# A channel shuffle on one core: copies on VectorE alone, program order, a small first tile and three small last ones

## The chip, the cores and the metric

The kernel runs on one core of a Trainium2 chip. The metric is the device time of one execution in microseconds (us), lower is better. All runs below are on one core at a granted clock of 1.0.

## The reference

Channels are regrouped: within each row of 256 channels, 8 groups of 32 are transposed to 32 groups of 8. Nothing is computed.

```python
# x: 16 x 64 x 64 x 256, float32; groups = 8
x = x.reshape(batch, h, w, groups, channels_per_group)
x = x.transpose(0, 1, 2, 4, 3)
return x.reshape(batch, h, w, c).astype(np.float32)
```

That is 65,536 rows of 1 KB: 67.11 MB to read and 67.11 MB to write.

## The kernel before

A tile gives each of the 128 partitions q rows, lying together in memory, so that a load or a store moves one run of q KB per partition: a 24-row tile is 3 MB in 128 descriptors of 24,576 bytes, an 8-row tile is 1 MB in 128 descriptors of 8,192 bytes. Loads are issued from SyncE (queue q1 in the profile), stores from ScalarE (queue q10). In between, the permuting copy is split evenly, the first half on VectorE (DVE), the second on ScalarE (ACT).

```python
_SIZES = [24] * 21 + [8]
_IN_BUFS = 4
_OUT_BUFS = 4
_SHARES = (("vector", 1), ("scalar", 1))
# ... (cut: pools, rows(), permute())
    first = 0
    for q in _SIZES:
        in_tile = in_pool.tile([P, biggest * c], F32, name="in_tile")
        nc.sync.dma_start(out=in_tile[:, : q * c], in_=rows(x_flat, first, q))
        out_tile = out_pool.tile([P, biggest * c], F32, name="out_tile")
        # ... (cut: for each engine of _SHARES, its rows of the tile)
                permute(engine, out_tile[:, cols], in_tile[:, cols])
        nc.scalar.dma_start(out=rows(out_flat, first, q), in_=out_tile[:, : q * c])
        first += P * q
```

## Time and profile before

| | before |
|---|---|
| time, median of 3 | 317.53 us (317.53 to 317.59) |
| span of the profile | 316.0 us |
| ACT busy, DVE busy | 119 us (38%), 65 us (21%) |
| bytes moved, rate over the span | 134.2 MB, 425 GB/s |
| DMA engines continuously occupied | from 1.7 to about 313.9 us |

The page of the kernel before shows the busy tenths of each of 40 slices of the span, and then the queues:

```profile
DVE  0440321303030303113030303031220303030310
ACT  1681624425160606243351606061533426060620
...
DMA  8999999999999999999999999999999999999996
...
## 3 DMA queue, kind: packets, MB, share of 16 engines
q1 hardware_dynamic: 3168, 67.11, 49.8%
q10 hardware_dynamic: 3168, 67.11, 49.3%
```

The two compute rows are mostly empty and the DMA row is full, so the 16 DMA engines bound the kernel, loads and stores taking half each. A packet of the profile has the size of one descriptor: each queue has 2,688 of 24,576 bytes (912 ns at the median), 128 of 8,192 bytes (309 ns), and 352 of 4 bytes (9 ns; in all as many as the semaphore updates by DMAs in the trace, 704: the "semaphore packets" of the prediction). So a DMA here has 128 with data and 16 of 4 bytes, and 22 DMAs make 3,168. The listing by form gives the copies, with busy time, mean ns of one, and idle time before them with what ended it:

```profile
L49 ACT COPY out_tile<-in_tile 128x3072 f32<-128x3072 f32 x21 | 115.7, 5510 | 180.3 <-DMA in_tile<-in_x_dram 180.3
L51 DVE COPY out_tile<-in_tile 128x3072 f32<-128x3072 f32 x21 | 64.2, 3058 | 231.6 <-DMA in_tile<-in_x_dram 231.6
```

Both engines wait for loads. A 24-row load takes its share of the DMA for 14.5 us, the slower copy 5.5 us. The end of the timeline (start us, duration, engine, what) shows how it drains:

```profile
292.64 5.43 ACT L49 COPY out_tile<-in_tile 128x3072 f32<-128x3072 f32 x1 [9.11 <-DMA in_tile<-in_x_dram]
...
302.35 1.94 ACT L49 COPY out_tile<-in_tile 128x1024 f32<-128x1024 f32 x1 [4.29 <-DMA in_tile<-in_x_dram]
302.41 2.25 ACTq L66 DMA_DIRECT2D out_dram<-out_tile  x2
```

The last load has come in at 302.3 us; the store of the tile copied at 292.6 to 298.1 us goes out only at 302.4, behind the issue of the next copy. Still the engines stay busy with stores to the end, as the windows view shows (window, its length, busy us of DVE, ACT and POOL with instructions, clock, DMA share, GB/s):

```profile
300.00:308.00 8.00, 1.09 (x1) 1.94 (x1) 0.00 (x0) 1.00 1.03 443
308.00:311.00 3.00, 0.00 (x0) 0.00 (x0) 0.00 (x0) 1.00 0.95 410
311.00:312.00 1.00, 0.00 (x0) 0.00 (x0) 0.00 (x0) 1.00 0.78 328
312.00:313.00 1.00, 0.00 (x0) 0.00 (x0) 0.00 (x0) 1.00 1.04 442
313.00:314.00 1.00, 0.00 (x0) 0.00 (x0) 0.00 (x0) 1.00 0.70 295
314.00:316.00 2.00, 0.00 (x0) 0.00 (x0) 0.00 (x0) 1.00 0.01 4
```

This view books a packet in the window in which it starts, so short windows swing (0.78, then 1.04); with each packet spread over its own duration the engines are 16 of 16 busy up to 313 us.

### The profile page before, as it was taken

What the parts mean: (1) busy time and instruction counts of PE and PEld (TensorE: products, weight loads), DVE (VectorE), ACT (ScalarE), POOL (GpSimd) and SP (SyncE); (2) the same over time, 40 slices, a digit from 0 to 9 for tenths busy, and PEclk for the clock granted to TensorE, in tenths of its full rate; (3) what the DMA queues carried; (4) which work ended last, traced back from release to release, by engine and by line L of the source; (5) the groups of instructions that cost most, each with busy time, mean ns of one, the idle gap of its engine ahead of it and who ended that gap; (6) DMA issues with size and microseconds to landing.
All of it is one profiled execution on the core that took longest, in us unless ns stands there. A gap on an engine that the chain in (4) does not pass through costs nothing.

```text
span 316.0 us, 236 instructions
## 1 busy us (share of the span) xinstructions
DVE 65.3 (21%) x22; ACT 118.9 (38%) x23; POOL 0.2 (0%) x4
## 2 busy tenths in 40 slices
DVE  0440321303030303113030303031220303030310
ACT  1681624425160606243351606061533426060620
POOL 0000000000000000000000000000000000000000
DMA  8999999999999999999999999999999999999996
GB/s 302 439 395 426 426 445 432 420 442 439 417 439 445 417 436 442 426 426 445 426 423 445 439 414 442 442 417 439 442 421 432 442 420 432 442 429 429 421 446 291
DMA packets 6337, 134.23 MB, mean 425 GB/s; under 512 B 704, under 2 KB 704, under 8 KB 704
## 3 DMA queue, kind: packets, MB, share of 16 engines
q1 hardware_dynamic: 3168, 67.11, 49.8%
q10 hardware_dynamic: 3168, 67.11, 49.3%
q14 instruction: 1, 0.01, 0.0%
HBM read 67.11 MB, written 67.11 MB: 425 GB/s over the span
## 4 chain that ended last, share of the span: by engine, by line
another core or an unknown queue 43%; DMA 32%; ACT 20%; ACTq 1%; issue 0%
DMA in_tile<-in_x_dram 32%; ACT out_tile L49 20%; ACTq L66 1%; ACTq L49 0%
## 5 line engine op out<-in xcount | busy, mean ns | idle before, releaser
L49 ACT COPY out_tile<-in_tile 128x3072 f32<-128x3072 f32 (+1 forms) x22 | 117.7, 5348 | 184.6 <-DMA in_tile<-in_x_dram 184.6
L51 DVE COPY out_tile<-in_tile 128x3072 f32<-128x3072 f32 (+1 forms) x22 | 65.3, 2968 | 238.3 <-DMA in_tile<-in_x_dram 238.3
L49 ACT ACT_TABLE_LOAD x1 | 1.3, 1283 | 0.7 <-PEq L84 0.7
L84 POOL MEMSET const-bfloat16-1.0<- 128x1 bf16 x1 | 0.1, 102 | 0.0
L84 POOL MEMSET const-uint8-127<- 128x1 uint8 x1 | 0.1, 102 | 0.0
L84 POOL MEMSET const-float32-1.0<- 128x1 f32 x1 | 0.1, 99 | 0.0
L84 POOL MEMSET const-float32-0.0<- 128x1 f32 x1 | 0.1, 98 | 0.2 <-issue 0.2
## 6 DMA issues: line engine op xcount, KB each, us to landing
in_tile<-in_x_dram SPq DMA_DIRECT2D x21, 3072.0 KB, 52.6
out_dram<-out_tile ACTq DMA_DIRECT2D x21, 3072.0 KB, 20.2
in_tile<-in_x_dram SPq DMA_DIRECT2D x1, 1024.0 KB, 47.9
out_dram<-out_tile ACTq DMA_DIRECT2D x1, 1024.0 KB, 10.4
```

What stands on the lines that cost most here:

```text
L49: nc.scalar.copy(out=dst, in_=src)
L51: getattr(nc, engine).tensor_copy(out=dst, in_=src)
L66: nc.scalar.dma_start(out=rows(out_flat, first, q), in_=out_tile[:, : q * c])
L84: nc = _bacc.Bacc("TRN2", target_bir_lowering=False, num_devices=1)
```

## The change

The intent: ScalarE, which also issues the stores, is freed of copies; every store is issued right after its own copy; a small first tile starts the copies and stores sooner; and small last tiles shorten the drain. The whole diff:

```diff
-_SIZES = [24] * 21 + [8]
+_SIZES = [8] + [24] * 20 + [8, 8, 8]
-_SHARES = (("vector", 1), ("scalar", 1))
+_SHARES = (("vector", 1),)
@@
+    ctx.enter_context(tc.manual_schedule(engines=None))
     first = 0
     for q in _SIZES:
```

The line with `manual_schedule` is the one for the order. There are 48 DMAs in place of 44.

## The prediction

> **What bounds the kernel now.** The DMA engines. The page's slice row shows them at 8 or 9 tenths in every slice but the last, 425 GB/s over the span. Packet by packet, the trace has the 16 engines occupied from 1.7 us to about 313.9 us of a 316.0 us span. A 24,576-byte descriptor (one partition of a 24-row tile) takes 912 ns at the median, loading or storing: 24,576 x 16 / 912 ns = 431 GB/s. The 134.2 MB at that rate are 311 us. The rest is 1.7 us ahead of the first packet, about 1.6 us of slow load packets (each engine's first takes 1.4 to 2.2 us, and a patch near 18 to 22 us runs long), and about 1.5 us after the last store. [...]
>
> The compute engines wait: by form, ACT COPY of 128x3072 takes 5.51 us and DVE 3.06 us, x21 each; in the waits DVE idles 238 us and ACT 185 us for loads. A tile comes every 14.5 us (timeline), so copies are hidden. The chain of waits names ACT for 20%, but the DMA is busy beneath it: worth nothing.
>
> **What the change does.**
> - Removes the ACT copies (118 us) and the 1.3 us table load; DVE takes whole tiles. From its 1.095 us for 1024 elements and 3.02 us for 3072, 0.94 ns per element: about 5.9 us for 6144, 2.05 us for 2048 (estimates). The copy phase goes from 5.43 to 5.9 us inside a 14.5 us period: off the critical path. DVE total about 126 us, 40%.
> - Order. Before, the program puts two ACT copies ahead of two store issues, so every other store, ready 9 us sooner, is issued just after the next copy has started (65.5 to 74.5 us). After, each store follows its own copy. Queueing is shorter, but the queues had work anyway: 0 us.
> - First tile: lands after about 5 us instead of 11.0, first store about 9 us earlier. But the engines are busy with queued loads then: 0 us.
> - Last tiles: the final tile is 8 rows in both. From 302 to 314 us before, stores alone fill the engines. After, I estimate that some 10 us of stores are still queued when loading ends, against about 4 us to land, copy and issue the last tile: no gap, 0 us.
> - 48 DMAs for 44. An 8-row tile has 8,192-byte descriptors at 309 ns: three take 927 ns instead of 912. One 24-row tile cut in three, 8 descriptors per engine, both ways: 8 x 15 ns x 2 = 0.24 us; more 9 ns semaphore packets add 0.04 us. All on the critical path: +0.3 us.
>
> **Prediction.** 317.53 + 0.3 = 317.8 us; 8 in 10 between 317.2 and 318.6. Chances: faster by over 2% 0.01, within 2% 0.97, slower 0.02.
>
> **What would show it.** DMA still 8 or 9 tenths in all middle slices, mean 424 to 426 GB/s; 24,576-byte packets still at 912 ns; DVE COPY 128x6144 at 5.8 to 6.0 us x20; no ACT copy; one store issue after each copy; median landing of stores under 20.2 us; last store packet within 1 us of before's.
>
> **What would make it wrong.** A gap in the DMA row near the end, if stores have run down when the last loads land (some us); packets slower or faster under the more even mix of loads and stores (1% would be 3 us); the slow patch near 20 us going away or growing (0.7 us either way). A different DVE rate is harmless below 14 us.

The sum stands as 317.53 + 0.3 = 317.8 us.

## The result, and the profile after

The changed kernel took 318.53 us (median of 6, 318.35 to 318.63) against 317.56 (6 runs, 317.53 to 317.80) beside it. The ratio is 1.0028, 95% interval 1.0015 to 1.0041. (Ratios here are the mean of one kernel's fast runs over the mean of the other's of the same rounds, so not quite the ratio of the medians.) A second set of five, run later as an experiment, gave 318.42 us and 1.0025. So it is slower by 0.25 to 0.28%: small, but clear of zero.

The page after, in the parts that answer to those above:

```profile
DVE  2256153442607071524426170716244261707222
...
DMA  8999999999999999999999999999999999999996
...
## 3 DMA queue, kind: packets, MB, share of 16 engines
q1 hardware_dynamic: 3456, 67.11, 49.8%
q10 hardware_dynamic: 3456, 67.11, 49.3%
```

ACT has gone and the DMA row has not changed. The 288 more packets per queue are the two additional DMAs of 144 each. By form, DVE now has:

```profile
L51 DVE COPY out_tile<-in_tile 128x6144 f32<-128x6144 f32 x20 | 113.8, 5692 | 170.1 <-DMA in_tile<-in_x_dram 170.1
L51 DVE COPY out_tile<-in_tile 128x2048 f32<-128x2048 f32 x4 | 8.1, 2024 | 20.1 <-DMA in_tile<-in_x_dram 20.1
```

Its 5.69 us per tile is hardly more than ACT's half took before, and it waits for loads still. The difference is at the end. Timeline:

```profile
295.44 2.04 DVE L51 COPY out_tile<-in_tile 128x2048 f32<-128x2048 f32 x1 [4.02 <-DMA in_tile<-in_x_dram]
305.17 2.01 DVE L51 COPY out_tile<-in_tile 128x2048 f32<-128x2048 f32 x1 [7.68 <-DMA in_tile<-in_x_dram]
310.12 2.02 DVE L51 COPY out_tile<-in_tile 128x2048 f32<-128x2048 f32 x1 [2.94 <-DMA in_tile<-in_x_dram]
```

and the same stretch in windows (no ACT column, as ACT does nothing):

```profile
300.00:308.00 8.00, 2.01 (x1) 0.00 (x0) 1.00 0.96 409
308.00:311.00 3.00, 0.88 (x1) 0.00 (x0) 1.00 1.01 426
311.00:312.00 1.00, 1.00 (x1) 0.00 (x0) 1.00 0.41 172
312.00:313.00 1.00, 0.15 (x1) 0.00 (x0) 1.00 0.00 0
313.00:314.00 1.00, 0.00 (x0) 0.00 (x0) 1.00 1.07 451
314.00:316.00 2.00, 0.00 (x0) 0.00 (x0) 1.00 0.74 299
```

From about 311.6 us most DMA engines have nothing to do, and from 312.1 to 313.0 none has: the DMA share falls to 0.00 while DVE ends the copy of the last tile and its store is issued. Packet by packet, the idle time after 290 us up to the end of the first engine to finish is 1.4 us, averaged over the engines; before it is none. The last load packet ends at 309.3 us. The tile is landed and the copy begins at 310.1, ends at 312.1, and the store's first packet starts at 313.0: 3.7 us. But only 2.3 us of stores were left at 309.3. (Stores that are "left" are those of the earlier tiles, in time of the 16 engines together, here and below.)

Why were so few left? The small loads came slowly. A DMA view between 286 and 304 us, in which two of the three 8-row loads run beside 24-row stores (packets, MB, share of the engines' time):

```profile
q10 hardware_dynamic: 254, 5.85, 75.5%
q1 hardware_dynamic: 266, 1.94, 25.5%
```

The queues have had about the same number of packets, 254 and 266, and so very different numbers of bytes. 309 ns of load against 912 ns of store is a share of 309 / (309 + 912) = 25%, and this is what the view shows. It holds the other way round too. From 14 to 20 us the small first tile's 8,192-byte stores run beside 24,576-byte loads, with as many packets again:

```profile
q1 hardware_dynamic: 80, 1.97, 76.0%
q10 hardware_dynamic: 80, 0.66, 25.8%
```

In mid-run of the same kernel, from 200 to 229 us, with 24,576 bytes on both sides, the shares are even:

```profile
q1 hardware_dynamic: 288, 6.29, 50.4%
q10 hardware_dynamic: 287, 6.27, 50.2%
```

### The profile page after: what moved, and what is told of

The parts are those of the page before. It is cut to its first block, busy times and chain, and to the rows that moved or that the text cites. A ratio compares the mean times of both kernels' runs of the same rounds, so it can differ in the third digit from the quotient of the medians.

```text
span 316.9 us, 178 instructions
## 1 busy us (share of the span) xinstructions
DVE 121.9 (38%) x24; POOL 0.2 (0%) x4
## 4 chain that ended last, share of the span: by engine, by line
another core or an unknown queue 39%; DMA 30%; DVE 29%; issue 0%; DVEq 0%; SPq 0%
DMA in_tile<-in_x_dram 30%; DVE out_tile L51 29%; DVEq L51 0%; SPq L57 0%
## 5 line engine op out<-in xcount | busy, mean ns | idle before, releaser
L51 DVE COPY out_tile<-in_tile 128x6144 f32<-128x6144 f32 (+1 forms) x24 | 121.9, 5080 | 190.2 <-DMA in_tile<-in_x_dram 190.2
## 6 DMA issues: line engine op xcount, KB each, us to landing
out_dram<-out_tile ACTq DMA_DIRECT2D x20, 3072.0 KB, 23.6
```

What stands on the lines that cost most here:

```text
L51: getattr(nc, engine).tensor_copy(out=dst, in_=src)
```

## The experiments

Theory A: each DMA engine alternates one descriptor of the load queue with one of the store queue. The starts of the packets in the profile after look like it: 16 load packets start between 297.07 and 297.44 us, 16 store packets between 297.38 and 297.75, each 306 ns after one of those loads, and load packets again from 298.28. (The packets carry no engine number here, so this is read from their starts.) At the end, small loads therefore get a quarter of the time, the large stores three quarters; the stores run out before the last tile is in, and the hole in the DMA row follows. Its rivals: B, the small first tile leaves too little lead; C, program order or VectorE alone; D, the small copies and stores, or the number of DMAs. Runs e1 to e4 ran on one chip, beside 9 runs of the kernel before with median 317.73 us; e5 to e8 together on one chip, beside 11 with median 317.67. All results were correct.

### e1_big_last: no small last tiles

```diff
-_SIZES = [8] + [24] * 20 + [8, 8, 8]
+_SIZES = [8] + [24] * 21
```

> The changed kernel with sizes [8] + [24] x 21: small first tile, no small last ones, 44 DMAs. Theory A (the extra time over the 0.3 us of descriptors is a 1.5 us hole in the DMA row at 312 to 313 us, which is there because the three last loads have 8,192-byte descriptors, each engine alternates one load and one store descriptor, so these loads get a quarter of the time and the stores run down): no loads of small descriptors at the end, so no hole of over 0.5 us, the 16 engines busy to the last store; 317.3 to 317.9 us. Rival B (the small first tile leaves the loads with less lead over the stores for the whole run, and the tail is short of stores for that): the hole stays or is longer, since the last copy is now 5.7 us instead of 2.0; 319 us or more. Rival C (program order and VectorE alone cost it, whatever the sizes): 318.3 to 318.7 as after.

317.24 us (317.15 to 317.38), ratio 0.9988 (0.9975 to 1.0000). No hole to speak of (0.1 us); the last load packet ends at 298.8 us and stores fill the rest. This although the last copy takes 5.7 us:

```profile
300.11 5.68 DVE L51 COPY out_tile<-in_tile 128x6144 f32<-128x6144 f32 x1 [8.82 <-DMA in_tile<-in_x_dram]
```

It was just enough: 7.9 us of stores were left at 298.8, and the last tile's store began 7.9 us later. B has fallen: the small first tile is there and does no harm.

### e2_old_sizes: VectorE and program order, the old sizes

```diff
-_SIZES = [8] + [24] * 20 + [8, 8, 8]
+_SIZES = [24] * 21 + [8]
```

> VectorE alone and program order with the old sizes [24] x 21 + [8]: the copy and order parts of the change by themselves. Theory A: one small last load only, over 6 us of stores are left when it ends, no hole; 317.3 to 317.8 us, as before. Rival C: 318.3 or more.

317.57 us (317.29 to 317.87), ratio 0.9997 (0.9985 to 1.0010): as before. No hole; 10.4 us of stores are left when the last load ends. C has fallen: moving the copies and the order of the stores costs nothing.

### e3_new_sizes_only: both engines and the old order, the new sizes

```diff
 # against the kernel before
-_SIZES = [24] * 21 + [8]
+_SIZES = [8] + [24] * 20 + [8, 8, 8]
```

> The kernel before (both engines, its own order of issues) with the new sizes alone. Theory A: the three small last loads again take a quarter of the engines' time against 24-row stores; a hole of at least 1.5 us near the end, longer than after's if the second-last store is held back behind the last copy; 318.3 to 321 us. Rival C: no hole, 317.8 us (the descriptors' 0.3 us alone).

317.85 us (317.65 to 318.29), ratio 1.0007 (0.9993 to 1.0021). By its time alone this does not differ from the kernel before. There is a hole, but one of 0.8 us and not of 1.5 or more; my expectation was wrong about its size and about the sign of what the old order does to it. Windows of this run (DVE, ACT, POOL):

```profile
308.00:309.00 1.00, 0.00 (x0) 0.00 (x0) 0.00 (x0) 1.00 0.95 401
309.00:310.00 1.00, 0.72 (x1) 0.89 (x1) 0.00 (x0) 1.00 0.12 49
310.00:311.00 1.00, 0.41 (x1) 1.00 (x1) 0.00 (x0) 1.00 1.07 451
```

The second-last store had been ready since 303.3 us, but is issued at 309.2 with the start of the last copies. Held back, it was still to be done when the last tile came in, and filled the engines while that tile was copied: the old order hides a part of the hole by accident.

### e4_cut_stores: the last large stores cut to small descriptors

The loads stay as the change has them. The stores of the last two 24-row tiles are cut.

```diff
+_CUT = (19, 20)  # their stores in three DMAs of 8 rows
-    for q in _SIZES:
+    for n_tile, q in enumerate(_SIZES):
@@
-        nc.scalar.dma_start(out=rows(out_flat, first, q), in_=out_tile[:, : q * c])
+        step = 8 if n_tile in _CUT else q
+        for r in range(0, q, step):
+            cols = slice(r * c, (r + step) * c)
+            nc.scalar.dma_start(out=rows(out_flat, first, q)[:, cols], in_=out_tile[:, cols])
```

> The changed kernel, but the stores of its last two 24-row tiles each go out as three DMAs of 8 rows, so that from about 286 us loads and stores both have 8,192-byte descriptors. Theory A: loads and stores then share the engines about 8 to 8 (not 4 to 12), the last load ends about 299 us instead of 309, over 8 us of stores are left then, the hole is gone, and the time falls although descriptors cost another 0.24 us: 317.7 to 318.2 us. Rivals B and C: the share of loads or the hole does not depend on the size of the store descriptors; 318.6 to 318.9 us (after plus 0.24).

317.68 us (317.55 to 318.08), ratio 1.0003 (0.9990 to 1.0015), although this program has four more DMAs than the changed kernel. The DMA view from 286 to 299 us:

```profile
q10 hardware_dynamic: 373, 2.79, 50.8%
q1 hardware_dynamic: 369, 2.76, 50.2%
```

As many packets from each queue again, and with equal descriptors an even share of bytes. The last load packet ends at 299.6 us in place of 309.3, 12.2 us of stores are left, and the hole is gone:

```profile
308.00:311.00 3.00, 0.00 (x0) 0.00 (x0) 1.00 1.01 426
311.00:312.00 1.00, 0.00 (x0) 0.00 (x0) 1.00 1.01 426
312.00:313.00 1.00, 0.00 (x0) 0.00 (x0) 1.00 1.03 434
```

Nothing about loads, copies or tile sizes was changed; what changed is the size of the descriptors that the loads alternate with.

### e5_after_again: the changed kernel once more

> The changed kernel once more, unaltered, on the same chip as the next three, to compare them directly: 318.3 to 318.7 us, a hole of about 1.5 us in the DMA row near 312 us.

318.42 us (318.37 to 318.59), ratio 1.0025 (1.0012 to 1.0038). The hole is 1.2 us here; 2.4 us of stores were left when the last load ended.

### e6_one_load_three_stores: small copies and stores, no small loads

```diff
-_SIZES = [8] + [24] * 20 + [8, 8, 8]
+_SIZES = [8] + [24] * 21
@@ the load of each tile is one DMA, as before; then
+        step = 8 if n_tile == len(_SIZES) - 1 else q
+        for r in range(0, q, step):
+            cols = slice(r * c, (r + step) * c)
+            out_tile = out_pool.tile([P, biggest * c], F32, name="out_tile")
+            permute("vector", out_tile[:, : step * c], in_tile[:, cols])
+            nc.scalar.dma_start(out=rows(out_flat, first, q)[:, cols], in_=out_tile[:, : step * c])
```

> Sizes [8] + [24] x 21 in program order on VectorE; the last tile is loaded by one DMA of 24 rows, but copied and stored in three pieces of 8 rows: the small tail for copies and stores without the small loads. Theory A: the loads keep 24,576-byte descriptors, so loads and stores share evenly to the end, over 10 us of stores are left when the last load ends, no hole; 317.2 to 317.7 us. Rival D (it is the three small copies and stores, or having 48 DMAs, that cost it, not the small loads): a hole or 318.3 us and more.

317.24 us (317.01 to 317.32), ratio 0.9986 (0.9974 to 0.9998). No hole:

```profile
311.00:312.00 1.00, 0.00 (x0) 0.00 (x0) 1.00 1.01 426
312.00:313.00 1.00, 0.00 (x0) 0.00 (x0) 1.00 1.00 426
```

Its four small copies and four small stores are those of the changed kernel; only the last three loads are one. D has fallen. It is the fastest version here that is clear of the kernel before, by 0.14%; it does not differ from e1.

### e7_three_loads_one_store: the mirror

```diff
-_SIZES = [8] + [24] * 20 + [8, 8, 8]
+_SIZES = [8] + [24] * 21
@@
-        nc.sync.dma_start(out=in_tile[:, : q * c], in_=rows(x_flat, first, q))
+        step = 8 if n_tile == len(_SIZES) - 1 else q
+        for r in range(0, q, step):
+            cols = slice(r * c, (r + step) * c)
+            nc.sync.dma_start(out=in_tile[:, cols], in_=rows(x_flat, first, q)[:, cols])
```

> The mirror of the run before: the last 24-row tile is loaded by three DMAs of 8 rows into one buffer, copied whole and stored by one DMA. Bytes, copies and stores are those of the kernel with sizes [8] + [24] x 21 (317.24 us); only one load is cut. Theory A: the three loads get a quarter of the engines while 24-row stores last (to about 305 us), end at about 306 to 307 us instead of 299, and then a 5.7 us copy and about 1.4 us of landing and issue come with no store left: a hole of 6 to 7.5 us, 323 to 325 us. Rival D: cutting a load costs its descriptors only, 0.12 us; 317.2 to 317.7.

324.62 us (324.50 to 324.80), ratio 1.0220 (1.0207 to 1.0234). One load of 3 MB cut into three of 1 MB, with every byte, copy and store as in e1, costs 7.4 us (324.62 - 317.24; e6, of the same session as e7, also took 317.24). The shares from 286 to 304 us, and then the timeline's last copy:

```profile
q10 hardware_dynamic: 255, 5.87, 75.8%
q1 hardware_dynamic: 254, 1.92, 25.2%
```

```profile
307.48 5.68 DVE L51 COPY out_tile<-in_tile 128x6144 f32<-128x6144 f32 x1 [16.27 <-DMA in_tile<-in_x_dram]
```

The last tile is complete at 307.5 us; in e1 it was at 300.1. By then the stores are finished, and the engines idle while it is copied:

```profile
306.00:307.00 1.00, 0.00 (x0) 0.00 (x0) 1.00 0.66 279
307.00:313.00 6.00, 5.52 (x1) 0.00 (x0) 1.00 0.00 0
313.00:314.00 1.00, 0.16 (x1) 0.00 (x0) 1.00 0.00 0
```

The idle time is 7.2 us. This is the mechanism of the changed kernel, and its hole enlarged about five times, as the last copy takes 5.7 us in place of 2.0 and no stores are left.

### e8_rows_32: larger descriptors throughout

```diff
-_SIZES = [8] + [24] * 20 + [8, 8, 8]
-_IN_BUFS = 4
-_OUT_BUFS = 4
+_SIZES = [8] + [32] * 15 + [24]
+_IN_BUFS = 3
+_OUT_BUFS = 3
```

> A version meant to beat both: sizes [8] + [32] x 15 + [24], three buffers in and three out (the same bytes of SBUF), VectorE, program order, no small last tiles. From 912 ns for 24,576 bytes and 309 ns for 8,192 a descriptor costs about 7.5 ns beside its bytes; there are about 80 fewer per engine in both directions together, 0.6 us. If three buffers keep the loads ahead, no hole: 316.4 to 317.1 us. If three are too few, holes in the DMA row in mid-run and over 318 us.

317.07 us, but from 316.60 to 318.80 in six runs: three at 316.6 to 316.7, three at 317.45 to 318.8. The ratio is 0.9991 (0.9972 to 1.0011), so no gain is established. The profiled run was one of the quick ones (316.69) and has no hole; its 32,768-byte descriptors take 1,213 ns, so that the saving foreseen was there. What made the other three longer stays open; sizes and buffers were changed together here.

## Why the prediction was right or wrong

The time lay inside the stated range, near its upper end. "Within 2%" and the reason (full DMA engines; compute off the critical path) held. The size did not: +0.3 us was predicted, +0.97 measured. That the range held the time is in part luck: the sum missed a term, and two savings that nobody foresaw took 1.8 us of added work down to 0.9 us of span (below). The step that failed is "Last tiles: ... I estimate that some 10 us of stores are still queued when loading ends ... no gap, 0 us".

- **What bounds the kernel**: right. The 24,576-byte packets took 912 ns after as before, and the mean rate is 424 GB/s.
- **Copies off ACT, program order: 0 us**: right, shown by e2 (ratio 0.9997). VectorE took 5.69 us per tile, and not 5.9. The median landing of large stores was said to fall under 20.2 us; it rose to 23.6. A store that was held back before its issue (one copied by 65.5 us went out at 74.5 in the kernel before) now waits in the queue in place of that, and landing is counted from the issue: in e2, where the order and VectorE are all that differs, the median is 29.1 (23.4 in e1, with the small first tile). I had the sign of that sub-claim wrong; it costs nothing.
- **Small first tile: 0 us**: no cost, as e1 has it and is not slower than before. In e1 the load packets together took 0.3 us per engine less than in e2, as each engine's first, slow packet is a smaller one (the first 16 load packets take 1.4 to 2.2 us in the kernel before, and 0.6 to 1.2 us in the changed kernel, which has the same first tile as e1). The small gain may come from that; no run isolates it.
- **48 DMAs: +0.3 us**: the sign was right, the size is not resolved. All packets together took 313.4 us per engine before, and 313.8 (first profile) or 313.5 (e5) after, so +0.4 or +0.1.
- **Small last tiles: 0 us**: wrong. In the estimate I let loads and stores share the engines evenly in time, as they do in mid-run. Beside 24-row stores the 8-row loads got 25%, loading ended at 309.3 us and not at about 299, and 2.3 us of stores were left where I had put 10. The prediction named just this gap among the things that would make it wrong, and still put it at 0 in the sum. The other half of the estimate, "about 4 us to land, copy and issue the last tile", was right: 3.7 us. 3.7 less 2.3 is the hole of 1.4 us. e4 and e6 take it away by equal descriptors in two different ways, e7 enlarges it. The last store packet was to come within 1 us of before's; it came 1.3 us later.

The terms do not simply add up to the total. The hole (1.4) and the packets (0.4) make 1.8 us, and the mean end of the 16 engines moves by 1.7 us. But the last store packet ends only 1.3 us later (315.7 against 314.4), and the span is 0.9 us longer. One part is seen: after the hole all engines start together and finish within 0.2 us of each other, where before their ends were spread over 0.9 us. The stretch from the last packet to the end of the span also fell, from 1.5 to 1.2 us; why was not tested.

The prediction could have done better with its own trace. In the kernel before, the one 8-row load runs from 292 to 301 us beside a large store. The DMA view from 296 to 301 us:

```profile
q10 hardware_dynamic: 65, 1.60, 74.1%
q1 hardware_dynamic: 64, 0.50, 23.6%
```

The counts of packets are equal, 65 and 64, and the shares 74 to 24: with packets of unequal length, equal turns were unequal shares, and I did not look for that.

## What to carry to other kernels

Where loads and stores run at once on full DMA engines, each queue's share followed the size of its descriptors here: a small load beside large stores was slow (25% of the time for 8 KB against 24 KB), so that cutting the last loads delayed the tile on which the end depends (by 7.4 us in e7). It was the share and not the packets themselves: 8,192 bytes in 309 ns are 424 GB/s over 16 engines, 24,576 in 912 ns 431. If the drain is to be refined, keep the loads large and cut only copies and stores (e6), or cut both (e4). A smaller tail gains nothing (e6 took as long as e1) as long as the stores that are still queued cover landing, copying and issuing the last tile: compare these two times in the trace first.
